# A two-layer encoder trunk on one core: the y products of the delta-rule scan moved behind the scan into a third ring bank, operand copies on POOL, placing copies on ACT

## The chip, the cores and the metric

The kernel runs on one core of one Trainium2 chip, as one program in one launch. The metric is the device time of that launch in microseconds (us). A kernel is run several times and the median counts; the kernel before was run three times.

## The reference

Two layers of the same pattern work on 512 rows of width 1024, all in float32. What matters here is the order of the parts and the scan inside the mixing:

```python
for l in range(DEPTH):                                   # DEPTH = 2
    x = x + 0.5 * swiglu(rms_norm(x, norm_ffn1[l]), ...)
    h = rms_norm(x, norm_mix[l])
    proj = h @ w_in[l]                                   # RWKV | band attention | memory attention
    y_rwkv, v_first = rwkv7_time_mix(...)
    y_att = chunked_rel_attention(...)
    y_mem = memory_attention(...)
    merged = g_rwkv * (y_rwkv @ w_branch_rwkv[l]) + g_att * (...) + g_mem * (...)
    x = x + merged @ w_out[l]
    x = x + 0.5 * swiglu(rms_norm(x, norm_ffn2[l]), ...)
...
def step(state, inp):                                    # wkv7_scan, for each of 512 times and 8 heads of 64
    r_t, w_t, k_t, v_t, kk_t, b_t = inp
    sa = jnp.einsum('bhvk,bhk->bhv', state, kk_t)
    state = state * w_t[:, :, None, :] - sa[..., None] * b_t[:, :, None, :] + v_t[..., None] * k_t[:, :, None, :]
    return state, jnp.einsum('bhvk,bhk->bhv', state, r_t)
```

## The kernel before

**Tiles.** Activations lie transposed, features on the 128 partitions and the 512 times along the free axis. Each weight matrix comes in chunks of up to 1 MB (line 714, `load_w`): a DMA brings the raw float32, ACT sums its squares (`junk`), POOL adds over the partitions (`ar<-wm`), DVE makes a power-of-two scale from it (`qt`, `qs`, `qd`), and ACT and DVE write the chunk as two float16 parts (`wh`). Each big product is then three float16 matmuls; they read `hh`, `hl` (the normed x), `ab`, `ya`, `ym` or `yr`, and write PSUM banks named `g` and `as`. These are the big matmuls of the text.

**The mixing.** Line 995, `mixing`, runs four kinds of work beside each other: projections (line 1039), band attention (line 1103), memory attention (line 1186) and the scan (line 1277, `rwkv`). `rwkv` goes over four pairs of heads; with two layers there are eight passes. One pass has:

- a front that makes `ar` (kk and r with their decays), `be`, `ka` and `v`; two groups of 16 small products of these give `gx`, `g1` and the matrix `ut` that is to be inverted;
- transposes of `ut`, `be`, `ka`, `v` on PE (line 1258, `turned`), each into one PSUM bank, from which `placed` (line 1266) copies four blocks of 64x256 to `lab` (a tile tagged `kk`), to the two `kb` (tagged `kb0` and `be`) and to `vz` (tagged `ar`). The string `PL` (line 40) says for each of the four copies whether DVE or ACT makes it;
- four levels of doubling (line 1384) and a last half level, which turn `tt` into the inverse; each level has two groups of 16 products (line 1242, `each`);
- the scan proper over eight chunks of 64 times, one after the other. Each chunk needs three pairs of small products in the bank `xps` and, between them, short operations of DVE and ACT: the products `xps<-ar,gx`, a copy `cx`, the products `xps<-cx,tt`, the negated copies `vu`, the update products `xps<-kk,kb` and `xps<-ta,be`, and the new state in `vz`;
- for each chunk also the output y: four products into the bank `yp`, two from `vz` and `gx`, two from `vu` and `g1` (lines 1446 to 1451). Nothing in the scan reads y. After the last chunk y is normed (`s<-yp`, `w<-yp,m`), transposed, placed and gated.

Two kinds of plain copies prepare operands: `gx<-ar` (line 1370, two copies of 64x1024) ahead of the doubling, and `vu<-vz` (line 1417, two copies of 64x512, named `kk<-ar` and `ta<-ar` in the trace) ahead of the scan.

**PSUM.** There are eight banks: two for `g`, two for `as`, two in the ring `s` (line 595, taken by `rwkv` and the norms, strictly in the order of the program), one for `xps` and one for `yp`.

**What sets the order.** The kernel is recorded first. A planner (line 406, `run`) then schedules all operations of all engines with its own table of costs (line 232, `GROUPS`, and line 393) and writes each engine's instructions out in that order, so every engine runs a fixed list. Where the planner finds PE free for over 0.4 us, it puts in filling matmuls that nobody reads (`xps<-wt`, line 528). All instructions are issued from line 562; the profile therefore gives L562 for nearly all, and tiles tell them apart.

Of the kernel before, what the change touches and what calls it, by code (L numbers as in the profile page):

```python
# [6 lines left out]
F32 = mybir.dt.float32  # L7
# [6 lines left out]
PSUM = bass.MemoryType.PSUM  # L14
DRAM = bass.MemoryType.DRAM

P = 128
DM = 1024
T = 512
# [6 lines left out]
CH = 64  # L26
HV = ((0, 256), (256, 512))
NCH = T // CH
# [11 lines left out]
PL = "SVSVSVSVSVSVSVSVSSSSSVSV"  # L40
# [189 lines left out]
class Plan:  # L230
# [3 lines left out]
        4: {(128, CH, CH): 0.5},  # L234
        16: {(CH, CH, CH): 0.63, (CH, CH, P): 1.04, (CH // 2, CH // 2, CH // 2): 0.625},
# [344 lines left out]
def trunk(tc: tile.TileContext, i: dict, out: bass.AP, dbg: dict | None = None, depth: int = DEPTH):  # L580
    nc = tc.nc
    dbg = dbg or {}
    plan = Plan(tc)
    ctx = ExitStack()
    V, S, G, PE, D = plan.V, plan.S, plan.G, plan.PE, plan.D
# [9 lines left out]
    pq = ctx.enter_context(plan.pool(name="pq", bufs=2, space=PSUM))  # L595
    pa = ctx.enter_context(plan.pool(name="pa", bufs=2, space=PSUM))
    pc = ctx.enter_context(plan.pool(name="pc", bufs=1, space=PSUM))
# [4 lines left out]
    def nm(s):  # L602
        uid[0] += 1
        return f"{s}_{uid[0]}"
# [23 lines left out]
    def s_ps():  # L628
        return pq.tile([P, T], F32, tag="s", name=nm("s"))
# [294 lines left out]
    H2 = [slice(0, CH), slice(CH, P)]  # L924
    W2 = [slice(CH, P), slice(0, CH)]
# [69 lines left out]
    def mixing(l, pieces, kst):  # L995
# [281 lines left out]
        def rwkv():  # L1277
            for p in range(NP):
# [60 lines left out]
                g1 = tr("g1", [P, NCH, CH])  # L1339
                gx = tr("gx", [P, NCH, 2, 2 * CH])  # L1340
# [23 lines left out]
                for r, (a, b) in ((0, (slice(0, P), slice(0, P))), (1, H2), (1, H2[::-1])):  # L1364
                    o, x = parity(ti[a], r), parity(low[b], r)
                    V.tensor_tensor(out=o, in0=lev(C_EYE, 4)[b], in1=x, op=ALU.subtract)
                aw = small("aw", 8)
                for u, h in enumerate(H2):
                    o, x = gx[W2[u], :, u, :], ar[h].rearrange("p c a s -> p c (a s)")
                    V.tensor_copy(o, x)  # L1370
                    V.tensor_copy(aw[W2[u], :], ai[h, :, CH])
# [42 lines left out]
                yp = pc.tile([P, T], F32, tag="y", name=nm("yp"))  # L1414
                vu = [tr("kk", [P, NCH, CH]), tr("ta", [P, NCH, CH])]
                for u, h in enumerate(H2):
                    V.tensor_copy(vu[u][h], vz[h, :, u, :])
                    G.memset(vz[W2[u], 0, u, :], 0.0)
                for c in range(NCH):
# [26 lines left out]
                    with plan.block():  # L1446
                        ys = [yp[h, c * CH:(c + 1) * CH] for h in H2]
                        for u, o in enumerate(ys):
                            PE.matmul(o, lhsT=gx[:, c, u, CH:2 * CH], rhs=vz[:, c, u, :], start=True, stop=False)
                        for u, (o, w) in enumerate(zip(ys, W2)):  # L1450
                            PE.matmul(o, lhsT=g1[w, c, :], rhs=vu[u][w, c, :], start=False, stop=True)
# [22 lines left out]
                y = tm("yr", bufs=5)  # L1474
# [249 lines left out]
```

## Time and profile before

| what | value |
|---|---|
| median of 3 runs (range) | 2693.39 us (2689.6 to 2694.79) |
| the profiled execution's own time, and its span | 2695.39 us, 2693.6 us |
| mean granted clock of PE | 0.995 |
| busy PE, DVE, ACT, POOL (share of the span) | 99%, 61%, 57%, 4% |
| mixing, layer 0 and layer 1, without the first projections | 404 to 900 us, 1764 to 2226 us |

A row of the profile names the engine, the operation, the tiles as out<-in, and how often; a mean is that of one instruction. A float32 product is two instructions on PE, so a pair of products stands as x4. The ends of matmuls are modelled, since they are pipelined; how long a matmul really holds PE is read from the start of the next one. In the timeline the first number is the start, the second the duration, both in us. Rows of the list of waits give the total, the number and the longest wait.

### The profile page before, as it was taken

To read this page: it belongs to the slowest core of one execution; us is meant where nothing else is said; L and a number is where in the kernel's file an instruction comes from. 1 tells how busy PE (TensorE), PEld (TensorE's weight loads), DVE (VectorE), ACT (ScalarE), POOL (GpSimd) and SP (SyncE) were. 2 spreads that over 40 slices of the span, in tenths; PEclk is the share of its full clock that TensorE was granted. 3 is DMA by queue.
4 is the path that set the end of the run, shared out by engine and by line. 5 is a ranking of instruction groups with operands and counts; after the bars stand their busy time and mean duration, and the time that the engine had idled before them with its cause. 6 is when DMAs were issued, how large, how long until landed. Compare 5 with 4: busy or idle time off the path is not lost. (4 is left out here: it accounts for less than half of the span.)

```text
span 2693.6 us, 45695 instructions
## 1 busy us (share of the span) xinstructions
PE 2664.2 (99%) x18239; PEld 1440.6 (53%) x18239; DVE 1639.0 (61%) x4471; ACT 1528.3 (57%) x2543; POOL 109.2 (4%) x285
## 2 busy tenths in 40 slices
PE   9999999999999999999999999999999999999999
PEld 6444476655544465444574444755555444654445
DVE  6335478788776675354463444778877766843543
ACT  6556466665544666465464664666755446554642
POOL 0000000000000000000000000000000000000000
PEclk9999999999999999999999999999999999999999
DMA  4232342121212223322222223321211122223232
GB/s 174 94 110 91 117 157 76 64 72 36 79 55 72 94 94 118 110 94 102 102 96 109 94 106 120 123 72 60 76 39 69 67 80 102 95 94 110 94 110 79
DMA packets 47158, 249.37 MB, mean 93 GB/s; under 512 B 5312, under 2 KB 10688, under 8 KB 23648
## 3 DMA queue, kind: packets, MB, share of 16 engines
q1 hardware_dynamic: 46944, 246.45, 26.0%
q8 instruction: 143, 2.34, 0.3%
q14 instruction: 71, 0.58, 0.1%
HBM read 239.09 MB, written 7.34 MB: 91 GB/s over the span
## 5 line engine op out<-in xcount | busy, mean ns | idle before, releaser
L562 PEld LDWEIGHTS <-wh 128*128 128x128 f16 x10920 | 1052.4, 98 | 1012.8 <-issue 21.6
L562 PE MATMUL g<-hh,wh 128*128 128x512 f16 (+1 forms) x3216 | 980.1, 367 | 1.9 <-ACT hh L562 0.8
L562 ACT ACTIVATE wh<-wr,qs 128x1024 f16<-128x1024 f32 (+2 forms) x478 | 483.9, 1051 | 226.8 <-PE g L562 115.9
L562 ACT ACTIVATE junk<-wr 128x2048 uint8<-128x2048 f32 (+2 forms) x239 | 413.0, 1728 | 333.8 <-DMA wr<-ffn_in 145.8
L562 PE MATMUL g<-hl,wh 128*128 128x512 f16 (+1 forms) x1608 | 589.6, 367 | 0.2 <-DVE hl L562 0.2
L562 DVE SCALAR_TENSOR_TENSOR wh<-wr,qs,wh 128x1024 f16<-128x1024 f32 (+2 forms) x478 | 544.5, 1168 | 47.5 <-ACT wh L562 46.4
L562 PE MATMUL as<-hh,wh 128*128 128x512 f16 (+1 forms) x1536 | 443.3, 361 | 0.0
L562 PE MATMUL as<-hl,wh 128*128 128x512 f16 (+1 forms) x768 | 277.4, 361 | 0.0
L562 PE MATMUL as<-ab,wh 128*128 128x512 f16 (+1 forms) x1224 | 234.7, 350 | 0.0
L562 PE MATMUL g<-ab,wh 128*128 128x512 f16 (+1 forms) x1224 | 234.5, 350 | 0.0
L562 POOL PARTITION_ALL_REDUCE ar<-wm x239 | 95.9, 401 | 2382.8 <-ACT junk L562 2209.4
L562 DVE SCALAR_TENSOR_TENSOR a<-as,md,sg 128x512 f32<-128x512 f32 x44 | 33.0, 750 | 214.0 <-PE as L562 211.1
L562 DVE SCALAR_TENSOR_TENSOR a<-g,md,sg 128x512 f32<-128x512 f32 x44 | 33.0, 750 | 213.8 <-PE g L562 209.6
L562 DVE SCALAR_TENSOR_TENSOR x<-g,md,x 128x512 f32<-128x512 f32 (+1 forms) x62 | 39.0, 628 | 117.5 <-PE g L562 117.4
L562 DVE SCALAR_TENSOR_TENSOR x<-as,md,x 128x512 f32<-128x512 f32 (+1 forms) x62 | 38.9, 628 | 115.5 <-PE as L562 115.4
L562 DVE TENSOR_SCALAR qt<-ar 128x1 int32<-128x1 int32 x253 | 37.7, 150 | 103.2 <-POOL ar L562 101.2
L562 ACT ACTIVATE ti<-s 64x256 f32<-64x256 f32 (+1 forms) x144 | 54.3, 377 | 63.4 <-PE s L562 47.3
L562 ACT ACTIVATE sq<-x 128x256 f32<-128x256 f32 x96 | 37.0, 408 | 80.1 <-DVE x L562 51.2
L562 PE MATMUL xps<-wt 128*128 128x320 f16 x423 | 70.5, 316 | 5.5 <-DVE cx L562 3.1
L562 DVE SCALAR_TENSOR_TENSOR ab<-a,qs,ab 128x512 f16<-128x512 f32 x88 | 60.7, 746 | 9.5 <-ACT ab L562 9.5
L562 ACT ACTIVATE sg<-as,md 128x512 f32<-128x512 f32 x44 | 30.1, 683 | 56.3 <-PE as L562 56.2
L562 ACT ACTIVATE sg<-g,md 128x512 f32<-128x512 f32 x44 | 30.1, 684 | 54.5 <-PE g L562 54.4
(344 smaller groups left out, 3027.7 us busy)
## 6 DMA issues: line engine op xcount, KB each, us to landing
wr<-ffn_in SPq DMA_DIRECT2D x88, 1024.0 KB, 4.8
wr<-ffn_outa SPq DMA_DIRECT2D x32, 1024.0 KB, 4.8
wr<-w_gate SPq DMA_DIRECT2D x24, 1024.0 KB, 4.9
wr<-w_in SPq DMA_DIRECT2D x22, 1024.0 KB, 4.8
wr<-ffn_outb SPq DMA_DIRECT2D x16, 768.0 KB, 4.4
wr<-w_branch SPq DMA_DIRECT2D x24, 512.0 KB, 3.7
wr<-mem_kv SPq DMA_DIRECT2D x8, 1024.0 KB, 4.8
wr<-w_out SPq DMA_DIRECT2D x8, 1024.0 KB, 4.8
```

The source lines that it names most:

```text
L562: f(*[x.real() if isinstance(x, View) else x for x in a], **{y: x.real() if isinstance(x, View) else x for y, x in k.items()})
```

## The change

Four edits go together.

1. The y products leave the scan's loop. They stand behind it as one block: first the 16 from `vz` and `gx`, then the 16 from `vu` and `g1`, all into one bank. Only the first chunk's products start the bank anew.
2. y's bank is taken from the ring `s`, which has three banks now; the bank `yp` is gone. In the new program the y products are named `s<-ar,gx`, `s<-kk,g` and `s<-ta,g`.
3. The copies `gx<-ar` and `vu<-vz` are issued on POOL instead of DVE.
4. `PL` holds only S, so ACT makes all four placing copies at every place. At `ti` (inside the levels) it did so before; at the other five places DVE made two of four.

The planner's table gets a cost for a group of 32. Since the planner orders the whole program anew, the order changes on every engine, in both mixings.

```diff
-PL = "SVSVSVSVSVSVSVSVSSSSSVSV"
+PL = "SSSSSSSSSSSSSSSSSSSSSSSS"
...
+        32: {(128, CH, CH): 2.3},
...
-    pq = ctx.enter_context(plan.pool(name="pq", bufs=2, space=PSUM))
+    pq = ctx.enter_context(plan.pool(name="pq", bufs=3, space=PSUM))
...
                     o, x = gx[W2[u], :, u, :], ar[h].rearrange("p c a s -> p c (a s)")
-                    V.tensor_copy(o, x)
+                    G.tensor_copy(o, x)
...
-                yp = pc.tile([P, T], F32, tag="y", name=nm("yp"))
                 vu = [tr("kk", [P, NCH, CH]), tr("ta", [P, NCH, CH])]
                 for u, h in enumerate(H2):
-                    V.tensor_copy(vu[u][h], vz[h, :, u, :])
+                    G.tensor_copy(vu[u][h], vz[h, :, u, :])
...
-                    with plan.block():
-                        ys = [yp[h, c * CH:(c + 1) * CH] for h in H2]
-                        for u, o in enumerate(ys):
-                            PE.matmul(o, lhsT=gx[:, c, u, CH:2 * CH], rhs=vz[:, c, u, :], start=True, stop=False)
-                        for u, (o, w) in enumerate(zip(ys, W2)):
-                            PE.matmul(o, lhsT=g1[w, c, :], rhs=vu[u][w, c, :], start=False, stop=True)
+                yp = s_ps()
+
+                with plan.block():
+                    for c in range(NCH):
+                        for u, h in enumerate(H2):
+                            PE.matmul(yp[h, c * CH:(c + 1) * CH], lhsT=gx[:, c, u, CH:2 * CH], rhs=vz[:, c, u, :], start=(c == 0), stop=False)
+                    for c in range(NCH):
+                        for u, (h, w) in enumerate(zip(H2, W2)):
+                            PE.matmul(yp[h, c * CH:(c + 1) * CH], lhsT=g1[w, c, :], rhs=vu[u][w, c, :], start=False, stop=(c == NCH - 1))
```

**PE, layer 0, first pair of heads, third chunk of the scan, before.** The `xps` rows are the state's update, the `yp` rows are y, `g` is a projection:

```order
L562 MATMUL g_5511<-hh_2569,wh_5282 128x512
L562 MATMUL xps<-kk_5272,kb_1015_4119 64x64
L562 MATMUL xps<-ta_5197,be_4791 64x64
L562 MATMUL yp_294<-ar_4747,gx_4122 64x64 x2
L562 MATMUL yp_294<-kk_5272,g_1002_4123 64x64
L562 MATMUL yp_294<-ta_5197,g_1002_4123 64x64
L562 LDWEIGHTS wh_5282
```

The same pass after, at the end of its scan; `as` is attention, `s` is y's bank:

```order
L563 MATMUL as_5870<-con,sc_5699 128x2 x4
L563 MATMUL s_5222<-ar_4745,gx_4122 64x64 x16
L563 MATMUL s_5222<-kk_5196,g_1002_4123 64x64
L563 MATMUL s_5222<-ta_5114,g_1002_4123 64x64
...
L563 LDWEIGHTS wh_5629
L563 MATMUL g_5649<-hh_2569,wh_5629 128x512
```

Eight groups of four products, most of them right behind an update, became one group of 32; the last two rows of products stand eight times in turn.

**DVE, layer 0, second pair of heads, the placing copies of `ut` (to `kk`) and of `be` and `ka` (to `kb` and `be`), before.** Each DVE copy waits for ACT's copy out of the same bank or for PE:

```order
L562 COPY kk_6280<-s_6371 64x4x64 [waits PE_49]
L562 COPY kk_6280<-s_6371 64x4x64 [waits Activation_49]
L562 TENSOR_TENSOR tt_5821<-ti_5329,con 128x512
L562 COPY be_6396<-s_6383 64x4x64 [waits Activation_49]
L562 COPY kb_1113_5774<-s_6383 64x4x64 [waits Activation_49]
L562 COPY kb_1113_5774<-s_6398 64x4x64 [waits PE_49]
L562 COPY be_6396<-s_6398 64x4x64 [waits Activation_49]
```

After, ACT holds all of them (`wh` is a weight chunk, `ya` an attention output):

```order
L563 ACTIVATE kk_6291<-s_6363 64x4x64 [waits PE_49]
L563 ACTIVATE kk_6291<-s_6363 64x4x64 x3
L563 ACTIVATE kb_1113_5798<-s_6415 64x4x64 [waits PE_49]
L563 ACTIVATE be_6438<-s_6415 64x4x64 x2
L563 ACTIVATE kb_1113_5798<-s_6415 64x4x64
L563 ACTIVATE wh_6333<-wr_5856,qs_5578 128x512
L563 ACTIVATE ya_4102<-as_6424 128x512 [waits PE_49]
```

The waits between DVE and ACT are gone there, and DVE's list has none of these copies.

**POOL, layer 0, first pair of heads, after.** `ISA` is the sum over partitions for a weight chunk's scale:

```order
L563 ISA ar_4231<-wm_4157 128x1 [waits DVE_49,Activation_49]
L563 COPY gx_4122<-ar_4126 64x8x128 [waits DVE_49,PE_49,Pool_49]
L563 COPY gx_4122<-ar_4126 64x8x128
L563 ISA ar_4265<-wm_4228 128x1 [waits Activation_49,Pool_49]
L563 MEMSET ar_4745 64x64 [waits PE_49,Pool_49]
L563 MEMSET ar_4745 64x64
L563 ISA ar_4397<-wm_4390 128x1 [waits Activation_49,Pool_49]
L563 ISA ar_4449<-wm_4443 128x1 [waits Activation_49]
L563 COPY ta_5114<-ar_4745 64x512 [waits DVE_49,PE_49,Pool_49]
L563 COPY kk_5196<-ar_4745 64x512 [waits PE_49]
L563 ISA ar_4649<-wm_4647 128x1 [waits Activation_49,Pool_49]
```

Before, the same stretch of POOL's list held the sums and the two clearings (`MEMSET`) alone; the four copies now stand between the sums of later weight chunks.

## The prediction

> **What bounds the kernel now.** I read the page first, then the two mixings, 404 to 900 us and 1764 to 2226 us, by windows: once for all instructions, once for the filling matmuls `xps<-wt` alone.
>
> ```profile
> span 2693.6 us, 45695 instructions
> PE 2664.2 (99%) x18239; PEld 1440.6 (53%) x18239; DVE 1639.0 (61%) x4471; ACT 1528.3 (57%) x2543; POOL 109.2 (4%) x285
> ...
> 404.00:900.00 496.00, 483.86 (x4554) 272.84 (x4552) 380.72 (x1191) 283.12 (x597) 15.64 (x44) 0.99 0.19 65
> 1764.00:2226.00 462.00, 454.77 (x4370) 253.55 (x4370) 365.34 (x1121) 269.52 (x575) 16.30 (x41) 0.99 0.19 64
> ...
> 404.00:900.00 496.00, 13.03 (x73) 7.01 (x73) 0.00 (x0) 0.99 0.19 65
> 1764.00:2226.00 462.00, 8.05 (x50) 4.64 (x50) 0.00 (x0) 0.99 0.19 64
> ```
>
> The columns of the windows are length, then busy time and instructions of PE, weight loads, DVE, ACT and POOL; the last two rows (filling matmuls) have PE, weight loads and DVE only. PE is the bound, in the mixings as elsewhere: it stands idle there 496.00 - 483.86 = 12.1 us and 462.00 - 454.77 = 7.2 us, and another 13.0 + 8.1 = 21.1 us go to 123 matmuls that nobody reads, 0.171 us each. So of 958 us of mixing some 40 us wait for something, and the rest is work of PE. DVE is busy 380.72 / 496 = 77%, ACT 57%, POOL 3%. A gain can come in two ways: PE gets less to do, or the waits shrink. I expect the first, and little of the second.
>
> **The y products.** What they hold PE is read from the starts of PE's rows in the timeline.
>
> ```profile
> 484.50 0.27 PE L562 MATMUL xps<-kk,kb 128*64 128x64 f32 x1 [0.18 <-ACT kk L562]
> ...
> 484.67 0.29 PE L562 MATMUL yp<-ar,gx 128*64 128x64 f32 x4
> 484.89 0.27 PE L562 MATMUL yp<-kk,g 64*64 64x64 f32 x1
> ...
> 485.15 0.44 PE L562 MATMUL as<-con,sc 128*128 128x128 f32 x2
> ...
> 485.68 0.34 PE L562 MATMUL xps<-ar,gx 128*64 128x64 f32 x4
> 485.95 0.23 PE L562 MATMUL g<-wh,hh 128*128 128x128 f16 x1
> ...
> 637.96 0.38 PE L562 MATMUL g<-hl,wh 128*128 128x512 f16 x1
> 638.17 0.38 PE L562 MATMUL g<-hh,wh 128*128 128x512 f16 x1
> 638.48 0.34 PE L562 MATMUL yp<-ar,gx 128*64 128x64 f32 x4
> ...
> 639.01 0.39 PE L562 MATMUL g<-hh,wh 128*128 128x512 f16 x1
> ...
> 452.52 0.69 PE L562 MATMUL s<-tt,ta 64*64 64x64 f32 x32
> 453.15 0.39 PE L562 MATMUL g<-hh,wh 128*128 128x512 f16 x1
> ...
> 404.00:900.00 496.00, 18.34 (x256) 13.01 (x256) 5.50 (x8) 0.99 0.19 65
> 1764.00:2226.00 462.00, 18.27 (x256) 12.85 (x256) 5.47 (x8) 0.99 0.19 64
> ```
>
> Behind an update, update and y together take 485.15 - 484.50 = 0.65 us. A group of four small instructions by itself takes 485.95 - 485.68 = 0.27 us. So y costs 0.38 us there. Alone between big matmuls it costs 639.01 - 638.48 = 0.53 us, and 0.10 us more ahead of it, since 0.31 us instead of 0.21 us lie between the starts of the last big matmul and of y: 0.63 us. In the program's order 40 of the 64 groups stand behind an update and 24 do not: 40 x 0.38 + 24 x 0.63 = 30.3 us.
>
> The new block has 32 products, 64 instructions; two run at a time, on different halves of the array, so it has 32 steps. The trace has no such block. The nearest row is the doubling's group of 32 instructions, four at a time, eight steps, 453.15 - 452.52 = 0.63 us. Against the 0.27 us of two steps that is (0.63 - 0.27) / 6 = 0.06 us for each further step. Two starts and 28 further steps make 2 x 0.27 + 28 x 0.06 = 2.22 us, with 0.10 us ahead of it 2.32 us; eight passes, 18.6 us. **Saved: 30.3 - 18.6 = 11.7 us.** The bounds: if each step takes as long as from the first to the second of a group, 0.10 us, the block takes 0.54 + 2.80 + 0.10 = 3.44 us, eight of them 27.5 us, and 2.8 us are saved. If y really holds PE for the busy time of its own two rows above, 18.34 + 18.27 = 36.6 us, 18.0 us are saved. I take 11.7 us, because it rests on starts and not on modelled ends.
>
> This saving counts in full only if PE has other work ready where y stood. It has: in the order 39 of the 61 runs of y rows are followed directly by a big matmul, as in the two rows above.
>
> **The chain of a pass.** The scan passes follow one another through the ring, so what makes a pass longer matters where PE runs dry. The block ends 2.22 - 0.53 = 1.7 us later behind the last chunk than the last y group did, and the norm of y waits for that: up to 8 x 1.7 = 13.6 us against us. On the other side stand the copies that leave DVE.
>
> ```profile
> L562 DVE COPY gx<-ar 64x1024 f32<-64x1024 f32 x16 | 11.1, 694 | 0.4
> L562 DVE COPY w<-s 64x256 f32<-64x256 f32 x16 | 6.8, 427 | 7.5 <-ACT w L562 4.4 <-PE s L562 3.0
> ...
> L562 DVE COPY kb<-s 64x256 f32<-64x256 f32 x16 | 6.8, 425 | 2.7 <-ACT be L562 2.6
> L562 DVE COPY ta<-ar 64x512 f32<-64x512 f32 x8 | 3.4, 424 | 0.2
> ...
> L562 DVE COPY kk<-ar 64x512 f32<-64x512 f32 x8 | 3.4, 419 | 0.2
> ...
> L562 ACT ACTIVATE ar<-s 64x256 f32<-64x256 f32 x16 | 6.0, 373 | 2.4 <-PE s L562 1.8 <-DVE ar L562 0.4
> ...
> 648.70 0.42 DVE L562 COPY w<-s 64x256 f32<-64x256 f32 x1
> 649.16 0.38 ACT L562 ACTIVATE w<-s 64x256 f32<-64x256 f32 x1
> 649.57 0.43 DVE L562 COPY w<-s 64x256 f32<-64x256 f32 x1 [0.44 <-ACT w L562]
> ...
> 650.03 0.38 ACT L562 ACTIVATE w<-s 64x256 f32<-64x256 f32 x1 [0.49 <-DVE w L562]
> ```
>
> Five places with 16 DVE copies each (the first and the last are shown) make 34.0 us, with `gx` and `vu` 11.1 + 3.4 + 3.4 = 17.9 us: DVE loses 51.9 us of work, 6.5 us a pass. ACT gets 80 copies of 0.373 us, 29.8 us; at 57% it has room. The four rows of `w<-s` show what DVE's two copies were worth: copies out of one bank do not overlap. DVE, ACT, DVE, ACT go one after the other, 648.70 to 650.41, 1.71 us, each waiting for the one before. Four on ACT take 4 x 0.38 = 1.52 us. Giving all to ACT costs no time where ACT is free, and the waits on both sides go; what is queued behind them on ACT is the casting of weights, and it moves by the two more copies, 0.75 us.
>
> The ring's third bank goes to y, which holds it from the block to the end of the norm's subtraction. What it frees is the start of the next pass: that used to wait until y was turned and placed, and now first needs y's bank back. I take the chain as shorter by less than one us a pass: -2.2 us of DVE copies (two `gx`, two `vu`: 17.9 / 8) and -0.4 us at the two places on the chain (`kk`, `w`), against +1.7 us. On PE's waits I put **-2 us** in all; the bounds are +13.6 us (only the block's late end counts) and -19.3 us (all idle time goes).
>
> **The filling matmuls.** In the new order layer 0's mixing has 33 of them instead of 73, layer 1's 94 instead of 50 in the same stretch: +4 in all, 4 x 0.171 = **+0.7 us**. So the planner's own gaps do not vanish; they move from layer 0 to layer 1.
>
> **The copies on POOL.** No trace row shows a copy on POOL.
>
> ```profile
> L562 POOL MEMSET ar<- 64x64 f32 x16 | 2.3, 145 | 59.0 <-PE s L562 42.0 <-DVE qd L562 8.3 <-issue 4.2
> ...
> 594.71 0.66 PE L562 MATMUL s<-con,tt 128*128 128x128 f32 x4
> ...
> 601.38 0.27 PE L562 MATMUL xps<-kk,kb 128*64 128x64 f32 x1
> ...
> 550.93 1.39 DVE L562 COPY gx<-ar 64x1024 f32<-64x1024 f32 x2
> ...
> 564.15 0.78 ACT L562 ACTIVATE ar<-s 64x256 f32<-64x256 f32 x2
> ...
> L562 PEld LDWEIGHTS <-wh 128*128 128x128 f16 x10920 | 1052.4, 98 | 1012.8 <-issue 21.6 <-DVE wh L562 1.8
> ```
>
> From below I bound it by DVE's rows, 0.694 and 0.42 us, from above by POOL's clearing of 64 elements in 145 ns, scaled: 2.3 us for 1024 elements, 1.16 us for 512. In all that is 16 x 0.694 + 16 x 0.42 = 17.8 us to 16 x 2.3 + 16 x 1.16 = 55.4 us of POOL. I take the upper end, the same engine. Both pairs are covered. `vu` can be copied once the products with `lab` are done, at 594.71, and the first update needs it at 601.38: 6.7 us for 2.3 us. The tile `ar` that `gx` reads is overwritten by the placed v, on ACT, at 564.15, 13.2 us after 550.93, for 4.6 us; if that cover went, ACT would stand in front of its weight casts until POOL is through. The sums for weight scales behind the copies come up to 4.6 us later; weight loads waited only 1.8 us for `wh` in the whole run, so that is hidden too. I put **0 us**; the price without cover is in the first rival. [...]
>
> **The sum.** 2695.4 us, the profiled execution's own time, - 11.7 - 2 + 0.7 + 0 = 2682.4 us. The median of the runs shown, 2693.4 us, is 2.0 us below that execution, so I say **2681 us** for a median.
>
> **Rivals.**
>
> *POOL's copies hold DVE up (slower).* DVE is busy 77% of the mixings, so nearly every copy on POOL meets DVE at work. If DVE's operations on SBUF must stand while POOL copies, DVE is late in lumps of up to 4.6 us in the front of a pass (`gx`) and 2.3 us ahead of the scan (`vu`), 55.4 us in all; less the 17.9 us that the same copies took of DVE before, 37.5 us of lateness. PE's list is fixed, so what of that PE's next small product sees becomes waiting. At three fifths it is 22 us, and the time 2703 us. It decides for slower from 11 + 6.7 = 18 us that reach PE, 2.2 us a pass. For it: the chain's operations right behind `gx` run on DVE. Against it: the operations of DVE that read a PSUM bank and one tile may pass, and many of the chain's do; the sum of DVE's work would not exceed what it is now. [...]
>
> *The freed time only turns into waits (no change).* If the passes' chain and not PE's work sets the mixings' length, y lay in time that PE had anyway, and 11.7 us come back as idle time or filling: 2693 us, or a few us more by the block's late end. For it: the rows of filling, and the 0.18 us wait for `kk` ahead of 484.50. Against it: the big matmuls right behind y.
>
> *Layer 1's new order is worse than its count (about no change).* It has 44 more fillings, 7.5 us, that layer 0 must give back. If layer 0 gives back only half, 3.4 us (20 x 0.171) are lost, and if layer 1 then waits as much again beside its fillings as the 7.2 us that it has now, the time is 2681 + 3.4 + 7.2 = 2692 us.
>
> That the change does not do what it says has one form: the third bank is y's, so the ring gives the other steps hardly more room than before. That is in the sum.
>
> **How the numbers follow.** The forecast has 0.57, POOL 0.20, the freed time as waits 0.13, layer 1 0.10. A measurement of this kernel tells about 0.2%, 5.4 us, from no change. Faster by more than that (under 2688): the forecast and half of the layer 1 case, 0.62. Within: the waits and the other half, 0.18. Slower: 0.20. The range goes from 2667 us (y saves its 18.0 us, and 8 us of the waits go) to 2702 us, which holds nearly half of the POOL case; about 0.10 above and 0.07 below are left out.
>
> **What would show it.** Right: the y rows begin 32 steps within 2.1 to 2.4 us, eight times; both mixings together are 10 to 16 us shorter, layer 0 by more than layer 1; PE's idle time in them stays about 19 us. DVE's busy time falls by about 52 us, ACT's rises by 30 us, and no placing copy waits for the other engine. Wrong: DVE's rows beside a POOL copy get longer or start late behind it (first rival); the idle time and the fillings grow by what y saved (second); layer 1's mixing is longer than 462 us (third). A block of over 3.4 us would undo the main term by itself.

## The result, and the profile after

The changed kernel takes **2673.52 us** (median of 4 runs, 2672.80 to 2673.89), the kernel before 2691.49 us (4 runs, 2688.72 to 2694.79). The ratio is 0.9932, 95% interval 0.9920 to 0.9944: 18.0 us less, where 12.4 us were predicted.

The head of the page after; the columns are those of before, and instructions are issued from line 563 (L563) here:

```profile
span 2671.0 us, 45730 instructions
...
PE 2642.8 (99%) x18243; PEld 1431.2 (54%) x18243; DVE 1595.2 (60%) x4359; ACT 1557.4 (58%) x2623; POOL 145.8 (5%) x317
```

The span is 22.6 us shorter, PE's busy time 21.4 us; that is 4.6 us more than the medians differ, since the profiled execution of before took 2695.4 us and lies above its median, and the one of after took 2672.8 us. Differences read from the two traces carry this. DVE has 43.8 us less, ACT 29.1 us more, POOL 36.6 us more.

The two mixings by windows. A program that orders its work anew shifts every time, so the edges are set here by PE's own list: layer 0 from the start of the 1908th big matmul to that of the 3588th, layer 1 from the 7836th to the 9600th. First the kernel before, all instructions, then its filling matmuls (PE, weight loads and DVE only):

```profile
390.34:898.24 507.90, 495.76 (x4668) 284.20 (x4666) 392.62 (x1251) 292.52 (x618) 17.43 (x48) 0.99 0.20 68
1721.07:2245.65 524.58, 516.93 (x4747) 290.28 (x4744) 410.38 (x1276) 311.01 (x646) 20.34 (x51) 0.99 0.20 69
...
390.34:898.24 507.90, 12.62 (x70) 6.72 (x70) 0.00 (x0) 0.99 0.20 68
1721.07:2245.65 524.58, 11.39 (x72) 6.80 (x72) 0.00 (x0) 0.99 0.20 69
```

The same stretches of the changed kernel:

```profile
390.82:875.17 484.35, 478.46 (x4634) 274.62 (x4633) 366.47 (x1188) 306.02 (x655) 36.76 (x63) 1.00 0.21 71
1697.17:2224.29 527.12, 513.61 (x4790) 290.99 (x4789) 390.56 (x1220) 325.90 (x685) 37.47 (x67) 1.00 0.20 68
...
390.82:875.17 484.35, 5.92 (x36) 3.51 (x36) 0.00 (x0) 1.00 0.21 71
1697.17:2224.29 527.12, 18.55 (x116) 11.16 (x116) 0.00 (x0) 1.00 0.20 68
```

Layer 0 is 23.6 us shorter, layer 1 is 2.5 us longer; outside the mixings little changes. PE's idle time is the length less PE's busy time: before 12.1 + 7.7 = 19.8 us, after 5.9 + 13.5 = 19.4 us. The fillings are 142 before and 152 after. So both kinds of gap only moved from layer 0 to layer 1, as the prediction had it. The clock column rose from 0.99 to 1.00 in both, and that was not in the prediction.

The y block of the first pass on PE, from its first product to the first big matmul behind it:

```profile
521.80 1.15 PE L563 MATMUL s<-ar,gx 128*64 128x64 f32 x32
522.88 0.27 PE L563 MATMUL s<-kk,g 64*64 64x64 f32 x1
522.88 0.27 PE L563 MATMUL s<-ta,g 64*64 64x64 f32 x1
522.98 0.22 PE L563 MATMUL s<-kk,g 64*64 64x64 f32 x1
...
523.80 0.22 PE L563 MATMUL s<-kk,g 64*64 64x64 f32 x1
523.81 0.22 PE L563 MATMUL s<-ta,g 64*64 64x64 f32 x1
523.96 0.39 PE L563 MATMUL g<-hh,wh 128*128 128x512 f16 x1
```

It holds PE 523.96 - 521.80 = 2.16 us; the prediction had 2.22 us. From 522.98 on two products start every 0.06 us (14 steps to 523.80), which is the pace that was taken from the doubling's groups.

Where the clock was lost before: the windows of layer 0 about 728 us, the clock in the third column from the right, and PE's timeline beside it.

```profile
724.00:726.00 2.00, 2.00 (x19) 1.70 (x15) 1.53 (x11) 0.31 (x1) 0.00 (x0) 1.00 0.79 242
726.00:728.00 2.00, 0.66 (x6) 0.29 (x5) 1.83 (x8) 0.00 (x0) 0.00 (x0) 1.00 0.94 348
728.00:730.00 2.00, 0.69 (x6) 0.38 (x6) 0.73 (x4) 1.71 (x1) 0.00 (x0) 0.93 0.82 266
730.00:732.00 2.00, 1.41 (x5) 0.56 (x4) 0.53 (x4) 1.95 (x8) 0.38 (x1) 0.50 1.02 395
...
736.00:738.00 2.00, 2.00 (x12) 1.55 (x11) 0.22 (x1) 0.82 (x2) 0.00 (x0) 0.50 0.00 0
738.00:740.00 2.00, 2.00 (x5) 0.64 (x3) 0.00 (x0) 0.60 (x1) 0.00 (x0) 0.51 0.01 4
740.00:742.00 2.00, 2.00 (x19) 1.00 (x18) 1.34 (x4) 0.50 (x1) 0.00 (x0) 1.00 0.01 4
```

```profile
726.32 0.34 PE L562 MATMUL xps<-ar,gx 128*64 128x64 f32 x4
728.50 0.43 PE L562 MATMUL xps<-wt 128*128 128x320 f16 x2 [1.85 <-DVE cx L562]
728.87 0.33 PE L562 MATMUL xps<-cx,tt 64*64 64x64 f32 x4
730.59 0.69 PE L562 MATMUL xps<-wt 128*128 128x320 f16 x2 [1.39 <-ACT kk L562]
```

Here PE waits 1.85 us for `cx` and 1.39 us for `kk` with two fillings between, and from about 730 to 740 us the granted clock is 0.50: from 736 to 740 us PE is busy throughout and works at half speed; the products `as<-con,pt` from 735.99 us on start every 0.21 us, those at full clock every 0.11 us (median of 56). That the waits are paid a second time here, as slow work, is only read from this order of events. From 726.66 to 730.59 us PE is idle for 1.85 + 1.39 = 3.24 us, more than anywhere else in as short a time in before's two mixings; but behind the wait of 1.62 us that ends at 2036.95 us the clock stays at 1.00, and of the other three stretches at half clock one begins 1.2 us behind a wait of 0.54 us and two with no idle time in the 6 us ahead of them. In the records of the clock, stretches at 0.50 make up 23.9 us of the two mixings before and 3.4 us after.

The table adds up PE's rows from start to start over both mixings; what lies beyond a row's own end counts as idle, and time at half clock lies inside the other columns. "y + scan" is the products of y and those in the bank `xps`, and "rest" is big matmuls, attention and the other products of the scan's fronts. The experiments below use the same columns.

| kernel | median us | layer 0 | layer 1 | y + scan | fillings | idle | rest | at half clock |
|---|---|---|---|---|---|---|---|---|
| before | 2691.5 | 507.9 | 524.6 | 78.0 | 22.3 (142) | 19.8 | 912.4 | 23.9 |
| **after** | 2673.5 | 484.3 | 527.1 | 66.5 | 22.4 (152) | 19.4 | 903.2 | 3.4 |
| before's order, y collected | 2690.0 | 506.0 | 522.8 | 67.3 | 22.1 (142) | 30.0 | 909.5 | 10.2 |
| before's order, copies on ACT | 2698.1 | 509.0 | 529.8 | 78.1 | 23.8 (142) | 26.7 | 910.2 | 23.9 |
| after's order, y block twice | 2688.3 | 492.1 | 535.6 | 83.6 | 22.4 (152) | 20.4 | 901.3 | 0.0 |
| after's order, copies shared with DVE | 2704.0 | 501.1 | 545.5 | 66.5 | 22.4 (152) | 37.8 | 919.9 | 34.2 |
| after's order, `gx` and `vu` on DVE | 2672.7 | 484.4 | 527.1 | 66.6 | 22.4 (152) | 19.8 | 902.6 | 3.4 |
| copies on ACT, planned anew | 2675.6 | 491.7 | 526.4 | 77.8 | 13.9 (95) | 16.9 | 909.4 | 13.6 |
| that order, y collected | 2678.3 | 491.7 | 527.6 | 68.1 | 14.0 (95) | 24.5 | 912.8 | 13.6 |
| copies on ACT, POOL copies, planned anew | 2670.4 | 490.6 | 519.3 | 76.1 | 5.1 (34) | 20.2 | 908.5 | 3.4 |
| y behind the scan, planned anew | 2712.4 | 511.0 | 538.5 | 66.9 | 43.9 (293) | 29.4 | 909.4 | 17.0 |
| before, LIFT 100 | 2697.7 | 502.8 | 525.6 | 76.9 | 34.0 (233) | 13.8 | 903.7 | 6.8 |
| after, LIFT 100 | 2697.6 | 499.7 | 527.8 | 67.1 | 30.7 (207) | 23.6 | 906.1 | 17.0 |
| copies on ACT, LIFT 100 | 2687.8 | 499.3 | 524.3 | 77.6 | 18.5 (128) | 18.7 | 908.7 | 17.0 |

After against before: y and scan -11.5 us, fillings +0.1, idle -0.4, rest -9.2; together -21.0 us. The rest is the same work, and some 20.5 us less of it ran at half clock. At half speed such a stretch does half its work, so 20.5 / 2 = 10 us would be lost in it.

All columns but the median are of one execution each, and the last one varies among executions of one kernel. For the kernel before, 62 executions are on record beside the experiments: their mean granted clock goes from 0.993 to 0.999 and their time from 2696.9 to 2684.1 us, about 1.7 us for each 0.001 (straight line, correlation -0.88). Their mean clock is 0.996, and the profiled execution has 0.995; the four of the changed kernel have 0.998 or 0.999. By that line some 5 us of the 18.0 us between the medians go with the clock, an estimate; the 9.2 us belong to the two executions that were profiled.

### The profile page after: what moved, and what is told of

It is laid out like the page before. It is cut to its first block, busy times and chain, and to the rows that moved or that the text cites. A ratio compares the mean times of both kernels' runs of the same rounds, so it can differ in the third digit from the quotient of the medians.

```text
span 2671.0 us, 45730 instructions
## 1 busy us (share of the span) xinstructions
PE 2642.8 (99%) x18243; PEld 1431.2 (54%) x18243; DVE 1595.2 (60%) x4359; ACT 1557.4 (58%) x2623; POOL 145.8 (5%) x317
## 5 line engine op out<-in xcount | busy, mean ns | idle before, releaser
L563 PEld LDWEIGHTS <-wh 128*128 128x128 f16 x10920 | 1053.2, 98 | 1015.1 <-issue 21.8
L563 PE MATMUL g<-hh,wh 128*128 128x512 f16 (+1 forms) x3216 | 977.5, 367 | 1.7 <-DVE r L563 1.1
L563 ACT ACTIVATE wh<-wr,qs 128x1024 f16<-128x1024 f32 (+2 forms) x478 | 483.5, 1050 | 224.7 <-PE g L563 120.9
L563 ACT ACTIVATE junk<-wr 128x2048 uint8<-128x2048 f32 (+2 forms) x239 | 412.7, 1727 | 332.7 <-DMA wr<-ffn_in 146.4
L563 PE MATMUL g<-hl,wh 128*128 128x512 f16 (+1 forms) x1608 | 589.5, 367 | 0.2 <-DVE hl L563 0.2
L563 DVE SCALAR_TENSOR_TENSOR wh<-wr,qs,wh 128x1024 f16<-128x1024 f32 (+2 forms) x478 | 546.7, 1173 | 40.6 <-ACT wh L563 39.5
L563 PE MATMUL as<-hh,wh 128*128 128x512 f16 (+1 forms) x1536 | 443.3, 361 | 0.0
L563 PE MATMUL as<-hl,wh 128*128 128x512 f16 (+1 forms) x768 | 277.4, 361 | 0.0
L563 PE MATMUL as<-ab,wh 128*128 128x512 f16 (+1 forms) x1224 | 234.7, 350 | 0.0
L563 PE MATMUL g<-ab,wh 128*128 128x512 f16 (+1 forms) x1224 | 234.5, 350 | 0.0
L563 POOL PARTITION_ALL_REDUCE ar<-wm x239 | 98.9, 414 | 2191.0 <-ACT junk L563 2035.3
L563 DVE SCALAR_TENSOR_TENSOR a<-as,md,sg 128x512 f32<-128x512 f32 x44 | 33.0, 750 | 214.5 <-PE as L563 211.5
L563 DVE SCALAR_TENSOR_TENSOR a<-g,md,sg 128x512 f32<-128x512 f32 x44 | 33.0, 750 | 213.4 <-PE g L563 209.1
L563 DVE SCALAR_TENSOR_TENSOR x<-g,md,x 128x512 f32<-128x512 f32 (+1 forms) x62 | 39.0, 628 | 115.6 <-PE g L563 115.5
L563 DVE SCALAR_TENSOR_TENSOR x<-as,md,x 128x512 f32<-128x512 f32 (+1 forms) x62 | 38.9, 628 | 114.8 <-PE as L563 114.8
L563 DVE TENSOR_SCALAR qt<-ar 128x1 int32<-128x1 int32 x253 | 37.8, 150 | 105.1 <-POOL ar L563 102.9
L563 ACT ACTIVATE sq<-x 128x256 f32<-128x256 f32 x96 | 37.0, 407 | 80.6 <-DVE x L563 51.5
L563 PE MATMUL xps<-wt 128*128 128x320 f16 x427 | 70.3, 313 | 6.0 <-DVE ar L563 2.0
L563 ACT ACTIVATE ti<-s 64x256 f32<-64x256 f32 (+1 forms) x144 | 54.3, 377 | 30.4 <-PE s L563 19.6
L563 DVE SCALAR_TENSOR_TENSOR ab<-a,qs,ab 128x512 f16<-128x512 f32 x88 | 60.7, 746 | 9.4 <-ACT ab L563 9.4
L563 ACT ACTIVATE sg<-as,md 128x512 f32<-128x512 f32 x44 | 30.1, 683 | 56.2 <-PE as L563 56.2
L563 ACT ACTIVATE sg<-g,md 128x512 f32<-128x512 f32 x44 | 30.1, 684 | 54.1 <-PE g L563 54.1
```

Of the source, the lines that this page charges most:

```text
L563: f(*[x.real() if isinstance(x, View) else x for x in a], **{y: x.real() if isinstance(x, View) else x for y, x in k.items()})
```

## The experiments

The theory at the start was that of the prediction: y's smaller work on PE is the gain. Its rivals were that freed PE time turns into waits, and that the gain is the new order, whichever edit brought it about. Kernels that keep an order test this best: the planner then sees the old operations, and the change is made where its list is written out. Each ratio is to runs of the kernel before beside it.

### y collected behind the scan, everything else in before's order

The planner sees before's program; its y groups are held when the list is written, and come out together at the place of the last one.

```diff
+            held = {}
...
+                calls = o.calls
+                if o.yg:
+                    ys = held.setdefault(o.yg[0], [])
+                    ys.append(o)
+                    if len(ys) < NCH:
+                        continue
+                    ys.sort(key=lambda x: x.yg[1])
+                    calls = [x for y in ys for x in y.calls[:2]] + [x for y in ys for x in y.calls[2:]]
...
+                        plan.cur.yg = (l, p), c
-                            PE.matmul(o, lhsT=gx[:, c, u, CH:2 * CH], rhs=vz[:, c, u, :], start=True, stop=False)
+                            PE.matmul(o, lhsT=gx[:, c, u, CH:2 * CH], rhs=vz[:, c, u, :], start=(c == 0), stop=False)
...
```

> The order of before, kept on every engine; only the y products of a pass are collected and written out behind its last chunk, in the bank that they had. Fillers stay 123 in the two mixings. Work theory (y simply takes less of PE's time): about 11.5 us faster than before, 2680 us. Waits theory (y lay in time that PE had anyway): the idle time grows by as much, 2691 us, no change.

2690.02 us against 2691.76 us, ratio 0.9994 (0.9985 to 1.0002): no difference that can be told. The windows of both mixings, then what PE waited for in layer 0, before and in this kernel (total, times, longest; this kernel issues from line 571):

```profile
389.65:895.69 506.04, 489.14 (x4668) 279.59 (x4667) 392.01 (x1251) 292.47 (x618) 17.56 (x48) 0.99 0.20 68
1718.58:2241.43 522.85, 509.70 (x4746) 285.78 (x4745) 410.38 (x1276) 310.98 (x646) 20.29 (x51) 1.00 0.20 69
```

```profile
PE xps L562 <- DVE cx L562: 3.1, 2, 1.8
...
PE xps L562 <- ACT kk L562: 1.6, 2, 1.4
```

```profile
PE xps L571 <- DVE cx L571: 4.0, 3, 2.1
PE xps L571 <- DVE ar L571: 2.6, 7, 0.8
PE xps L571 <- ACT kk L571: 2.0, 3, 1.4
```

PE has 10.7 us less of y and scan, as calculated, and 10.2 us more of idle time: 16.9 + 13.2 us instead of 12.1 + 7.7. The y products had stood in front of the next chunk's products. Without them PE comes to `xps` too soon and waits for DVE's new state `ar`, seven times in layer 0 where before's list has no such wait, and eight times in layer 1: 2.6 us each, half of the added idle time. In this order the chain between PE, DVE and ACT takes back what y saves.

### y's block issued twice, in after's order

```diff
-        32: {(128, CH, CH): 2.3},
+        64: {(128, CH, CH): 2.3},
...
-                    for c in range(NCH):
-                        for u, h in enumerate(H2):
-                            PE.matmul(yp[h, c * CH:(c + 1) * CH], lhsT=gx[:, c, u, CH:2 * CH], rhs=vz[:, c, u, :], start=(c == 0), stop=False)
...
+                    for again in range(2):
+                        for c in range(NCH):
+                            for u, h in enumerate(H2):
+                                PE.matmul(yp[h, c * CH:(c + 1) * CH], lhsT=gx[:, c, u, CH:2 * CH], rhs=vz[:, c, u, :], start=(c == 0), stop=False)
...
```

> The order of after, with each pass's y block issued twice in a row (the second writes the same values again); the planner counts it once, so that nothing else moves. Work theory: eight more blocks of 2.16 us, 17.3 us slower than after, 2691 us. Waits theory: part of it disappears in idle time, under 9 us slower than after.

2688.31 us, ratio 0.9988 (0.9979 to 0.9997), 14.8 us over the changed kernel, for 83.6 - 66.5 = 17.1 us more of PE's work. In this order, work added at the end of a pass costs nearly its length. Together with the experiment before: time added to PE was paid here, and time taken from it was not given back there. What the changed kernel's own order would lose with y back in the loop was not run.

### Placing copies on ACT alone, planned anew

```diff
-PL = "SVSVSVSVSVSVSVSVSSSSSVSV"
+PL = "SSSSSSSSSSSSSSSSSSSSSSSS"
```

> Only the placing copies go to ACT; planned anew. The new order has 9 fillers in layer 0's mixing and 65 in layer 1's, against 73 and 50. Order theory (what the plan does to PE's gaps and clock decides beside y): 49 x 0.171 = 8.4 us less filling and some idle time with it, 2678 to 2684 us, nearly all of it in layer 0. Work theory (only y matters): no change, 2691 us.

2675.60 us, ratio 0.9942 (0.9930 to 0.9955): 16.2 us less, with y in the loop and its 77.8 us of y and scan untouched. This one edit, which the prediction had priced at 0.4 us a pass, gives nine tenths of the gain, more than either expectation. The fillings fall from 142 to 95, the idle time by 2.9 us, the time at half clock from 23.9 to 13.6 us (in an execution that took 2679.8 us, the longest of its five). Layer 0 is 16.2 us shorter, layer 1 is 1.8 us longer.

### y behind the scan alone, planned anew

y's block behind the loop as in the change, in its own bank `yp`; `PL`, ring and POOL as before.

```diff
+        32: {(128, CH, CH): 2.3},
...
-                    with plan.block():
-                        ys = [yp[h, c * CH:(c + 1) * CH] for h in H2]
...
+                with plan.block():
+                    for c in range(NCH):
+                        for u, h in enumerate(H2):
+                            PE.matmul(yp[h, c * CH:(c + 1) * CH], lhsT=gx[:, c, u, CH:2 * CH], rhs=vz[:, c, u, :], start=(c == 0), stop=False)
...
```

> Only y goes behind the scan, in its own bank; planned anew. The new order has 126 fillers in layer 0's mixing and 142 in layer 1's, against 73 and 50. Work theory: 11.5 us faster, 2680 us. Order theory: 145 x 0.171 = 24.8 us more filling against the 11.5 us, so 13 us slower than before or worse, 2705 us.

2712.40 us, ratio 1.0074 (1.0061 to 1.0086): 20.6 us slower; the order theory had 13 us or worse. PE's y and scan fall by 11.1 us here too. The planner finds an order with 293 fillings instead of 142 (+21.6 us), 9.6 us more idle time, and both mixings longer, by 3.1 and 13.9 us. The edit that the prediction took for the main term makes the kernel slower when it comes alone.

### Placing copies on ACT, in before's order

```diff
-                    V.tensor_copy(o, ps[H2[r], :, h, :])
+                    plan.note("V", "tensor_copy", lambda o, x: nc.scalar.activation(o, x, AF.Copy), (o, x), {})
```

> The order of before, kept; the DVE placing copies are issued on ACT at the places that they had. Relief theory (copies that wait for each other cost the chain, and ACT alone is quicker): most of the 16 us that the edit gave when planned anew, 2677 to 2682 us. Order theory (the gain came from the new plan, not from the copies): within 3 us of before, 2689 to 2695 us.

2698.12 us against 2691.32 us, ratio 1.0026 (1.0017 to 1.0036): 6.8 us slower, which neither expectation had. DVE's turn at each bank is gone, and nothing is won by that: ACT's list was made for two copies at a place. PE's waits for ACT go from about 6 to 19 us, those for DVE from 11 to 6 us (idle 26.7 us instead of 19.8). So it is not the copies by themselves that gain 16 us, but the order that the planner makes for them.

### Placing copies shared with DVE again, in after's order

The mirror image: after's order on every engine, with 80 of the copies issued on DVE at the place that they have in the list.

```diff
-PL = "SSSSSSSSSSSSSSSSSSSSSSSS"
+PL = "SVSVSVSVSVSVSVSVSSSSSVSV"
...
-                    V.tensor_copy(o, ps[H2[r], :, h, :])
+                    plan.note("S", "activation", lambda o, x, *a: nc.vector.tensor_copy(o, x), (o, ps[H2[r], :, h, :], AF.Copy), {})
```

> The changed kernel's order on every engine, with 80 of the placing copies issued on DVE again, so that each bank is copied out by ACT, DVE, ACT, DVE as before. Order theory: the 16 to 18 us come from the order that was planned for copies on ACT alone, and who makes the copies matters little, as with the kernel before's order and ACT's copies (2698.12 us, +6.8 against it): 2673 to 2680 us. Copy theory: the waits between DVE and ACT at each bank were what cost time, and their end is the gain: 2685 to 2692 us.

2703.95 us against 2692.13 us, ratio 1.0042 (1.0029 to 1.0055): 30.4 us slower than the changed kernel. Both theories had it below 2692 us. ACT's groups of placing copies, in the changed kernel and then here; the last columns are ACT's idle time ahead of them and what ended it (L1274 is the line from which DVE's copies are issued here):

```profile
L563 ACT ACTIVATE be<-s 64x256 f32<-64x256 f32 x32 | 12.1, 378 | 0.4
L563 ACT ACTIVATE ar<-s 64x256 f32<-64x256 f32 x32 | 12.1, 378 | 0.5
...
L563 ACT ACTIVATE w<-s 64x256 f32<-64x256 f32 x32 | 12.1, 377 | 16.7 <-PE s L563 16.4
L563 ACT ACTIVATE kk<-s 64x256 f32<-64x256 f32 x32 | 12.1, 377 | 6.0 <-DVE gx L563 2.9 <-PE s L563 2.8
```

```profile
L563 ACT ACTIVATE be<-s 64x256 f32<-64x256 f32 x16 | 6.0, 377 | 26.4 <-DVE be L1274 26.4
L563 ACT ACTIVATE ar<-s 64x256 f32<-64x256 f32 x16 | 6.0, 377 | 10.1 <-DVE ar L1274 9.9
L563 ACT ACTIVATE w<-s 64x256 f32<-64x256 f32 x16 | 6.0, 376 | 21.3 <-PE s L563 16.4 <-DVE w L1274 4.9
L563 ACT ACTIVATE kk<-s 64x256 f32<-64x256 f32 x16 | 6.0, 374 | 14.4 <-DVE kk L1274 8.7 <-DVE gx L563 2.9 <-PE s L563 2.8
```

ACT now waits 26.4 + 9.9 + 4.9 + 8.7 = 49.9 us for DVE's copy out of the same bank. DVE is busy in all of that time, 17 us of it with the copy waited for and the rest with other work that its list has in front; none of these waits is there in the changed kernel. PE's idle time goes from 19.4 to 37.8 us, its time at half clock from 3.4 to 34.2 us. That is the whole difference in the mixings, 35.2 us: idle +18.4 us and rest +16.7 us, and not one product more.

### The copies of `gx` and `vu` back on DVE, in after's order

```diff
+    def on_dve(o, x):
+        plan.note("G", "tensor_copy", nc.vector.tensor_copy, (o, x), {})
...
-                    G.tensor_copy(o, x)
+                    on_dve(o, x)
...
```

> The order of after, with the gx and vu copies issued on DVE at the places that POOL had. If POOL relieves the chain, this is slower than after by several us, 2676 to 2682 us. If POOL's copies cost DVE as much as they save (33 us of POOL, some of it while DVE stands), the same as after within 2 us, 2672 to 2675 us.

2672.70 us, ratio 0.9928 (0.9914 to 0.9941), the same as the changed kernel (0.9920 to 0.9944). POOL's rows in the changed kernel, then rows of its timeline about a `gx` copy, and one of its groups:

```profile
L563 POOL COPY gx<-ar 64x1024 f32<-64x1024 f32 x16 | 21.6, 1351 | 94.3 <-DVE ar L563 38.8 <-DVE rs L563 28.1 <-PE as L563 27.1
L563 POOL COPY ta<-ar 64x512 f32<-64x512 f32 x8 | 5.8, 725 | 55.9 <-PE s L563 41.2 <-DVE wh L563 13.4 <-POOL ar L563 1.1
...
L563 POOL COPY kk<-ar 64x512 f32<-64x512 f32 x8 | 5.2, 655 | 31.9 <-PE s L563 31.9
```

```profile
437.08 3.31 POOL L563 COPY gx<-ar 64x1024 f32<-64x1024 f32 x2 [3.40 <-DVE ar L563]
437.43 4.04 DVE L563 SCALAR_TENSOR_TENSOR wh<-wr,qs,wh 128x1024 f16<-128x1024 f32 x2
...
669.17 2.41 POOL L563 COPY gx<-ar 64x1024 f32<-64x1024 f32 x2 [16.11 <-DVE ar L563]
...
L563 DVE SCALAR_TENSOR_TENSOR wh<-wr,qs,wh 128x1024 f16<-128x1024 f32 x364 | 456.9, 1286 | 31.0 <-ACT wh L563 30.6
```

The third row is another pair of POOL copies, the last one the mean of all such casts of DVE, 1.286 us. Where they run beside each other, two casts take 4.04 us and two copies 3.31 us, instead of 2.57 us and 2.41 us. So they do hold each other up. DVE's operations that read a PSUM bank kept their length beside POOL's copies: four `sc<-as,rq,bias` from 551.12 us on took 0.47 to 0.48 us, with 0.475 us as the mean of all 64, and `k<-g,mo,t` at 670.26 us took 0.74 us, its mean. The price is small. DVE is busy 1603.8 us in this experiment, 17.8 us of it the copies, so 1586.0 us for the rest; in the changed kernel that rest takes 1595.2 us, 9.2 us more over the whole run, and none of it reaches PE: both mixings are as long to 0.1 us.

### y collected, in the order planned for copies on ACT

The collecting of y from the first experiment, added to the kernel with `PL` all S.

> The order of the kernel that has only the placing copies on ACT (2675.6 us), with the y products collected behind the scan on top, and nothing else moved. As with the order of before, y and the update hold PE some 11 us less. Waits theory: idle time takes nearly all of it back, 2673 to 2676 us. Work theory: 2664 us.

2678.29 us, ratio 0.9948 (0.9936 to 0.9961), against 2675.60 us without it. Again y and scan are 9.7 us less, and the idle time 7.6 us more. The time lies above the 2676 us of the waits theory, too. In neither of the two orders that were planned with y in the loop did collecting it gain anything that can be told.

### LIFT 100 instead of 110

`LIFT` (line 35) is a rule of the planner about how much earlier the scan's work is drawn. It was set to 100 in the kernel before, in the changed kernel, and in the kernel with `PL` all S: three pairs that differ in their orders.

```diff
-LIFT = 110
+LIFT = 100
```

> The kernel before with one number of its planner changed (LIFT 100 instead of 110), nothing of the work. The new order has 124 and 143 fillers in the two mixings against 73 and 50. Order theory: 144 x 0.171 = 24.6 us of filling more and some idle time, 2712 to 2722 us. If the order were of no weight: 2691 us.

> The changed kernel with LIFT 100 instead of 110, planned anew: 100 and 142 filling matmuls in the two mixings instead of 33 and 94, 115 more. If each filling costs its 0.171 us: +19.7 us, 2693 us. If they stand where PE would be idle or at half clock anyway, as with the kernel before at LIFT 100 (146 more fillings, +6.4 us): 2675 to 2683 us. If the gain was one lucky order out of many, the time comes back to that of the kernel before: 2690 us or more.

> The kernel before with all placing copies on ACT (2675.6 us, 9 and 65 fillings) at LIFT 100, planned anew: 51 and 71 fillings. If copies on ACT alone let the planner find a better order at any LIFT: 10 us or more below the kernel before at LIFT 100 (2697.7 us), so 2676 to 2687 us. If the one order at LIFT 110 was luck: within 6 us of 2697.7 us.

| LIFT | before | copies on ACT | all four edits |
|---|---|---|---|
| 110 | 2691.5 | 2675.6 | 2673.5 |
| 100 | 2697.7 | 2687.8 | 2697.6 |

The ratios of the second row are 1.0026 (1.0017 to 1.0035), 0.9985 (0.9976 to 0.9994) and 1.0017 (1.0008 to 1.0026). Copies on ACT gain 16 us in one row and 10 us in the other. The other three edits on top of them change the time by -2 us in one row (the intervals overlap) and +10 us in the other. All four edits gain 18 us in one row and 0.1 us in the other, though y and scan are 9.8 us shorter there, too (67.1 against 76.9). Before gets 144 more fillings (PE's instructions, 18239 to 18383), 91 of them in the stretches of the table. There 6.0 us of idle time and 17.1 us at half clock go, and the mixings are 4.1 us shorter with more fillings; outside the stretches, where the other 53 stand, the profiled execution is 6.4 us longer. The median is 6.4 us longer, not the 20 us or more of the order theory. The changed kernel gets 115 more, 55 of them in the stretches; there idle time (+4.2 us) and half clock (+13.6 us) grow as well, and the time rises by 24 us. So the number of fillings is no price by itself, and the changed kernel's 18 us do not survive a small change to the planner's rule: this is what was expected for one lucky order out of many.

### Copies on ACT and POOL, y left in the loop, POOL's copy at its measured price

```diff
-PL = "SVSVSVSVSVSVSVSVSSSSSVSV"
+PL = "SSSSSSSSSSSSSSSSSSSSSSSS"
...
-            return 0.1 + n / 298
+            return 0.18 + n / 1190
...
-                    V.tensor_copy(o, x)
+                    G.tensor_copy(o, x)
...
-                    V.tensor_copy(vu[u][h], vz[h, :, u, :])
+                    G.tensor_copy(vu[u][h], vz[h, :, u, :])
```

> Copies on ACT alone and the gx and vu copies on POOL, with the planner's price for a POOL copy put to the 0.18 us + 1 us per 1190 elements that the changed kernel's trace shows; y stays in the loop and in its own bank. Planned anew: 4 and 9 fillings instead of 9 and 65 without POOL. If a filling that goes gives its 0.171 us: 61 x 0.171 = 10.4 us less than 2675.6 us, 2665 us, the best version so far. If the wait behind it stays as idle time: 2672 to 2680 us.

2670.42 us, ratio 0.9919 (0.9905 to 0.9932): the lowest median of all, though its interval and that of the changed kernel (0.9920 to 0.9944) overlap, so that it cannot be called faster. It falls between the two expectations: fillings 8.8 us less than without POOL, half clock 13.6 to 3.4 us, but 3.3 us more idle time. It shows that the time of the changed kernel is had without y's block and without the ring's third bank.

## Why the prediction was right, and where it was not

The time lies within the range and on the forecast side, 2673.5 us against 2681 us. That the size came out near is in part luck. The main term is not given back in either order to which it was added alone, a term that was left out is nearly as large in the traces, and at LIFT 100 the same edits with nearly the same saving on y gain 0.1 us. The terms of the sum, against the two mixings of the table:

| term | predicted us | measured us |
|---|---|---|
| y's products (with what the scan's groups pay for standing alone) | -11.7 | -11.5 |
| PE's waits | -2 | -0.4 |
| fillings | +0.7 | +0.1 |
| copies on POOL | 0 | 0 (the kernel with them on DVE: -0.8, within both intervals) |
| half clock | no term | about -9 (rest: -9.2) |

The measured terms are those of the two profiled executions and add up to -21.0 us; between the medians it is -18.0 us, of which some 5 us go with the clock. Two slips in the sums change nothing: 2682.4 - 2.0 is 2680.4, not 2681 us, and the 18 us that decide for slower are 12.4 + 5.4, not 11 + 6.7.

1. **The block's size was right.** 2.16 us instead of 2.22 us, and start to start the y rows go from 16.2 + 16.4 us to 2 x 8.7 us. The scan's own groups got 3.8 us longer (45.4 to 49.2 us), since nothing stands directly behind an update any more; the prediction's subtraction of pairs had this in it.
2. **The step that failed: "This saving counts in full".** It rested on 39 of 61 y rows with a big matmul behind them. What counts is not what stands behind y but what comes next of the scan: a big matmul that is pulled forward by 0.4 us brings the next `xps` forward as well, and in before's order that waits for DVE. The runs gave -1.7 us (before's order; its interval, -4.0 to +0.5 us, holds zero) and +2.7 us (the order for copies on ACT; the intervals of the two kernels overlap) in place of -11.7 us. The second rival, freed time that only turns into waits, had 0.13 and describes y by itself in these two orders. That y's 11.5 us appear as a term in the changed kernel is accounting: another order without them reaches the same time.
3. **The placing copies were mis-sized.** The prediction read four copies out of one bank as 1.71 us against 1.52 us and priced their step at -0.4 us a pass. With the order held, ACT alone is 6.8 us worse in before's order and 30.4 us better in after's. Planned anew, it is worth 16 and 10 us at two settings of the planner. The copies fit an order, and the prediction had no term for the fit of an order.
4. **Half clock was left out.** The rows of before showed 0.99 in the clock column; a mean clock of 0.99 over 1032 us is 10 us of PE's full speed lost, nearly the main term. The prediction shows these rows and has no term for it.
5. **The first rival was right in its mechanism and wrong in its price.** DVE and POOL hold each other up, 9.2 us over the run instead of the 37.5 us that were feared, and the copies took 21.6 + 5.8 + 5.2 = 32.6 us of POOL instead of the 55.4 us taken. They have cover, so nothing of it reaches PE.
6. **The third rival was half right.** Layer 1 has 44 more fillings (6.3 us) and 5.9 us more idle time, which eat its share of y; it ends 2.5 us longer. Layer 0 gave 23.6 us, more than this could undo.

Of the signs named: the block is within 2.1 to 2.4 us, layer 0 gains more than layer 1, the idle time stays at 19.4 us, and ACT's busy time rises by 29.1 us. DVE's falls by 43.8 us instead of 52, 51.9 us less what POOL's copies stretch. Both mixings together are 21.0 us shorter, not 10 to 16, by the missing term. No placing copy waits for another engine's copy at its bank.

Two things stay open. The ring's third bank was not tried by itself; the last kernel shows only that the time is had without it. And why the planner finds better orders when DVE makes none of the copies was not tried. The planner does take ACT's and DVE's copies out of one bank as running side by side: `touch` (line 307 of the kernel before) lets a read wait for writes alone, while the rows of before show the copies one after the other, four in 1.71 us. That this is the reason is only argued.

## What to carry to other kernels

In a kernel whose order is planned, test an edit twice: with the order held, and planned anew. Held, it shows what the operation is worth; planned anew, what the order is worth, and that may be the larger number, with either sign. Before counting work taken from the busiest engine as time, look whether the next link of a chain through other engines is ready earlier too; and look in the records of the clock for busy stretches at half speed, with a wait ahead of them or without one: here they were 23.9 us of the two mixings before and 3.4 us after. Before calling a gain of a planned kernel the edit's own, move one number of the planner and measure the pair again.

## What the runs showed of the hardware that was not expected

**The clock can halve without a gap.** Two windows of the kernel before, about 518 us, and PE's timeline there (the last row is from layer 1):

```profile
516.00:518.00 2.00, 2.00 (x22) 1.88 (x22) 1.75 (x10) 0.43 (x2) 0.00 (x0) 1.00 0.25 37
518.00:520.00 2.00, 2.00 (x23) 1.83 (x20) 1.88 (x12) 0.00 (x0) 0.00 (x0) 0.52 0.58 225
```

```profile
513.21 2.33 PE L562 MATMUL as<-pt,vt 128*64 128x512 f32 x16
515.46 0.33 PE L562 MATMUL xps<-cx,tt 64*64 64x64 f32 x4
515.73 1.95 PE L562 MATMUL as<-con,sc 128*128 128x2 f32 x16
...
518.06 0.37 PE L562 MATMUL yp<-kk,g 64*64 64x64 f32 x1
...
1955.56 1.95 PE L562 MATMUL as<-con,sc 128*128 128x2 f32 x16
```

PE is busy 2.00 us of 2.00 us on both sides, and the clock falls from 1.00 to 0.52; the product at 518.06 takes 0.37 us instead of 0.27 us, and the next one of its kind starts 0.16 us behind it instead of 0.10 us. Ahead of the drop stand 16 products with only two columns each. Behind the like row at 1955.56 us the clock's records have a drop, too, at 1958.51 us; whether the narrow products have a part in it, no run tested. They are not enough by themselves: such a row of 16 stands 24 times in the mixings of the traces kept, and the clock falls within 6 us behind 7 of them. In the kernel with before's order and copies on ACT the row at 512.92 us is the same one, and the clock stays at 1.00 from 514 to 522 us. In the records of the clock the four stretches of the two mixings are 3.413, 10.240, 6.827 and 3.413 us long, one, three, two and one times 3.413 us. The starts lie on one grid, too: from 518.08 to 729.71, 1958.51 and 1999.47 us it is 62, 422 and 434 times 3.413 us. In the changed kernel's trace the grid lies 0.60 us later against the start of the span (its first stretch at half clock begins at 13.51 us, that of before at 12.91 us). That it lies elsewhere in each execution, and the same order is hit in one and spared in another, would fit the 62 executions, but is only argued.

**A copy on POOL takes, at its shortest, half as long again as on DVE, not three times as long.** The shortest took 0.60 us for 512 elements of a row and 1.04 us for 1024, so 0.18 us + 1 us per 1190 elements; DVE's took 0.42 and 0.69 us. The means on POOL were 0.69 and 1.35 us. What the prediction took, scaled from a clearing of 64 elements in 0.145 us, was about twice the shortest (2.3 and 1.16 us).
